# Column sum of a 32768 x 2048 matrix: folding each 8-row tile with wide adds, and a one-partition result

## The chip, the cores and the metric

The kernel runs on one core of one Trainium2 chip. The metric is the device time of one execution in microseconds (us), the median of several. The profile's *span* is the time from the first to the last instruction of one execution; in the profiled executions it is 1.8 to 1.9 us less than the time.

DVE is VectorE, ACT is ScalarE, PE is TensorE, SP is SyncE; "PEld" is PE's weight load, and ACTq and SPq are the queues on which ACT and SP issue transfers.

## The reference

```python
batch, seq, dim = 32, 1024, 2048          # float32

def reference(grad_output):
    return np.sum(grad_output, axis=(0, 1)).astype(np.float32)
```

The kernel has to read 268.44 MB and write 8 KB. A "row" below is one group of 128 x 2048 numbers: one row of 2048 in each of the 128 partitions of on-chip memory. There are 256 rows: 31 bulk tiles of 8, then a tail of 4 + 2 + 1, and a last row that is loaded in pieces.

## The kernel before

DVE adds the rows of a bulk tile to an accumulator one by one. The last five rows of the last bulk tile, and the tail, go to PE, which sums over partitions by a matmul with ones. PE's array is used as four groups of 32 columns, and the result comes out in four partitions.

```python
io_pool = ctx.enter_context(tc.tile_pool(name="io", bufs=3))   # three tiles of 64 KB a partition
# [cut]
for t in range(n_bulk):                                        # 31 tiles
    T = io_pool.tile([P, ROWS * D], fp32, tag="T", name=f"t{t}")
    nc.sync.dma_start(out=T[:], in_=src)                       # 8 MB
    on_pe = PE_ROWS_LAST if t == n_bulk - 1 else 0             # 5 in the last tile
    for j in range(ROWS):
        part = T[:, j * D : (j + 1) * D]
        if j >= ROWS - on_pe:
            sum_row(part)                                      # eight matmuls
        # [cut: t == 0 makes acc]
        else:
            nc.vector.tensor_add(out=acc[:], in0=acc[:], in1=part)
# [cut: the tail's 4, 2 and 1 rows by sum_row, acc after the first four]
for k in range(SPLIT):                                         # last row, 4 pieces of 512 columns
    nc.sync.dma_start(out=dst, in_=flat[row : row + P, k * W : (k + 1) * W])
    # [cut: four matmuls of 128 columns, one for each column group]
nc.scalar.copy(out=res[:, :n], in_=head[:])                    # pieces 0 to 2, copied early
nc.vector.tensor_copy(out=res[:, n:], in_=last[:])             # piece 3
rows = res[:].rearrange("(g r) c -> g r c", r=32)[:, 0, :]     # 4 partitions
nc.scalar.dma_start(out=o[:, : SPLIT - 1, :], in_=rows[:, :n].rearrange("g (k i) -> g k i", i=C))
nc.sync.dma_start(out=o[:, SPLIT - 1, :], in_=rows[:, n:])
```

## Time and profile before

| before | |
|---|---|
| time, median of 4 (range) | 630.51 us (630.03 to 630.67) |
| span of the profiled execution | 628.6 us |
| load queue's share of the 16 DMA engines' span | 98.9% |
| DVE busy | 555.0 us, 88% |

The table of DMA queues comes first. Its columns are the packets, the MB, and the time of the packets as a share of 16 engines' span. q1 carries the loads; "instruction" marks fetches of the engines' own programs.

```profile
...
## 3 DMA queue, kind: packets, MB, share of 16 engines
q1 hardware_dynamic: 5480, 268.44, 98.9%
q8 instruction: 2, 0.03, 0.0%
q14 instruction: 2, 0.02, 0.0%
q10 hardware_dynamic: 16, 0.01, 0.0%
...
```

The loads fill the DMA engines: their queue takes 98.9% of the engines' span. The groups of instructions by line (busy us and mean ns of one; then the idle time before them and what ended it) and the table of waits (us in total, times, longest) show DVE behind them:

```profile
...
L81 DVE TENSOR_TENSOR acc<-acc,t 128x2048 f32<-128x2048 f32 x241 | 552.4, 2292 | 34.9 <-DMA t<-in_grad_output_dram 27.7
...
```

```profile
...
DVE acc L81 <- DMA t<-in_grad_output_dram: 27.7, 30, 3.2
DVE acc L79 <- DMA t<-in_grad_output_dram: 21.8, 1, 21.8
...
```

DVE waits 27.7 + 21.8 = 49.5 us for loads. The timeline of DVE (start, length, then what it waited for) shows how. Three neighbouring bulk tiles:

```profile
...
139.03 18.57 DVE L81 TENSOR_TENSOR acc<-acc,t 128x2048 f32<-128x2048 f32 x8 [0.92 <-DMA t<-in_grad_output_dram]
159.30 18.57 DVE L81 TENSOR_TENSOR acc<-acc,t 128x2048 f32<-128x2048 f32 x8 [1.70 <-DMA t<-in_grad_output_dram]
178.65 18.57 DVE L81 TENSOR_TENSOR acc<-acc,t 128x2048 f32<-128x2048 f32 x8 [0.78 <-DMA t<-in_grad_output_dram]
...
```

Each starts with idle time that ends when its load lands, so the starts are landing times. The last bulk tile lands here:

```profile
...
605.31 6.95 DVE L81 TENSOR_TENSOR acc<-acc,t 128x2048 f32<-128x2048 f32 x3 [0.78 <-DMA t<-in_grad_output_dram]
...
```

And this is the end, in the timeline of all engines:

```profile
...
624.81 0.48 ACT L105 COPY res<-head 128x384 f32<-128x384 f32 x1 [622.79 <-PE head L50]
...
624.94 0.43 PE L50 MATMUL last<-tail,ones 128*32 128x128 f32 x8 [0.20 <-DMA tail<-in_grad_output_dram]
625.32 1.11 ACTq L108 DMA_DIRECT2D out_dram<-res  x1
625.44 0.29 DVE L106 COPY res<-last 128x128 f32<-128x128 f32 x1 [13.18 <-PE last L50]
625.75 0.66 SPq L111 DMA_DIRECT2D out_dram<-res  x1
...
```

The last load lands at 624.94, which releases PE. A copy of 0.29 us follows, and the last store is issued at 625.75.

The chain of work that ended last, as shares of the span by engine, lists DVE too:

```profile
...
DMA 69%; DVE 29%; issue 0%; SPq 0%; PE 0%; DVEq 0%
...
```

It has DVE because an add frees the buffer that the next load fills. That does not make DVE a limit: a load lands 39.4 us after its issue (median in the table of DMA issues), two tiles' time, so a whole tile is still queued when DVE frees a buffer.

### The profile page before, as it was taken

Reading aid. Unit: us, or ns where it says so; the run is one execution under the profiler, and the core shown is the slowest. Engines: PE = TensorE matmul, PEld = TensorE weight load, DVE = VectorE, ACT = ScalarE, POOL = GpSimd, SP = SyncE. Lnnn points to the kernel's source line nnn. Section 1 sums busy time; section 2 is a strip of 40 time slices with the busy share of each in tenths; the row PEclk is TensorE's granted clock in tenths of the full one; section 3 lists DMA queues with packets and bytes.
Section 4 is the critical chain, followed back from the end, with each engine's and each line's share of the span. In section 5 each row is a group of like instructions: output and inputs, shape, how many; then the busy total and the mean of one; then the engine's idle time right before and its main releaser. Section 6 shows DMA issues by size and latency. Waiting matters only on the chain.

```text
span 628.6 us, 874 instructions
## 1 busy us (share of the span) xinstructions
PE 16.2 (3%) x240; PEld 7.9 (1%) x240; DVE 555.0 (88%) x244; ACT 1.8 (0%) x2; POOL 0.2 (0%) x4
## 2 busy tenths in 40 slices
PE   0000000000000000000000000000000000000045
PEld 0000000000000000000000000000000000000022
DVE  0579999999899999999999999999999999999980
ACT  0000000000000000000000000000000000000000
POOL 0000000000000000000000000000000000000000
PEclk9999999999999999999999999999999999999999
DMA  9999999999999999999999999999999999999996
GB/s 400 404 463 404 463 409 459 400 467 401 463 404 463 404 463 404 463 404 463 404 463 404 463 404 463 404 463 401 467 400 467 400 467 400 467 400 467 400 418 256
DMA packets 5500, 268.50 MB, mean 427 GB/s; under 512 B 616, under 2 KB 632, under 8 KB 1144
## 3 DMA queue, kind: packets, MB, share of 16 engines
q1 hardware_dynamic: 5480, 268.44, 98.9%
q8 instruction: 2, 0.03, 0.0%
q14 instruction: 2, 0.02, 0.0%
q10 hardware_dynamic: 16, 0.01, 0.0%
HBM read 268.44 MB, written 0.01 MB: 427 GB/s over the span
## 4 chain that ended last, share of the span: by engine, by line
DMA 69%; DVE 29%; issue 0%; SPq 0%; PE 0%; DVEq 0%
DMA t<-in_grad_output_dram 63%; DVE acc L81 29%; DMA tail<-in_grad_output_dram 6%; SPq L97 0%; SPq L87 0%; PE last L50 0%; SPq L69 0%; DVE res L106 0%; DVEq L81 0%
## 5 line engine op out<-in xcount | busy, mean ns | idle before, releaser
L81 DVE TENSOR_TENSOR acc<-acc,t 128x2048 f32<-128x2048 f32 x241 | 552.4, 2292 | 34.9 <-DMA t<-in_grad_output_dram 27.7
L50 PE MATMUL head<-t,ones 128*32 128x384 f32 x40 | 6.5, 723 | 605.4 <-DMA t<-in_grad_output_dram 605.4
L79 DVE TENSOR_TENSOR acc<-t 128x2048 f32<-128x2048 f32 x1 | 2.3, 2291 | 21.8 <-DMA t<-in_grad_output_dram 21.8
L106 DVE COPY res<-last 128x128 f32<-128x128 f32 x1 | 0.3, 291 | 13.2 <-PE last L50 13.2
L50 PEld LDWEIGHTS head<-t,ones 128*32 128x32 f32 x40 | 1.8, 156 | 605.3 <-DVE acc L81 605.3
L50 PE MATMUL head<-tail,ones 128*32 128x384 f32 (+1 forms) x80 | 7.1, 428 | 3.6 <-DMA tail<-in_grad_output_dram 3.6
L50 PE MATMUL last<-tail,ones 128*32 128x128 f32 x64 | 3.2, 274 | 0.2 <-DMA tail<-in_grad_output_dram 0.2
L50 PE MATMUL last<-t,ones 128*32 128x128 f32 x40 | 2.9, 362 | 0.0
L105 ACT COPY res<-head 128x384 f32<-128x384 f32 x1 | 0.5, 478 | 622.8 <-PE head L50 622.8
L50 PEld LDWEIGHTS head<-tail,ones 128*32 128x32 f32 x80 | 2.0, 109 | 4.9 <-DMA tail<-in_grad_output_dram 4.9
L50 PEld LDWEIGHTS last<-tail,ones 128*32 128x32 f32 x64 | 2.0, 110 | 3.2 <-issue 2.7
L50 PEld LDWEIGHTS last<-t,ones 128*32 128x32 f32 x40 | 1.9, 150 | 3.4 <-issue 3.4
L105 ACT ACT_TABLE_LOAD x1 | 1.3, 1283 | 0.7 <-PEq L126 0.7
L50 PE MATMUL head<-acc,ones 128*32 128x384 f32 x8 | 0.8, 486 | 0.0
L39 DVE MEMSET ones<- 128x32 f32 x1 | 0.1, 85 | 0.8 <-PEq L126 0.8
L50 PE MATMUL last<-acc,ones 128*32 128x128 f32 x8 | 0.4, 273 | 0.0
L50 PEld LDWEIGHTS last<-acc,ones 128*32 128x32 f32 x8 | 0.3, 110 | 0.4 <-issue 0.4
L50 PEld LDWEIGHTS head<-acc,ones 128*32 128x32 f32 x8 | 0.2, 110 | 0.0
L126 POOL MEMSET const-bfloat16-1.0<- 128x1 bf16 x1 | 0.1, 102 | 0.0
L126 POOL MEMSET const-uint8-127<- 128x1 uint8 x1 | 0.1, 102 | 0.0
L126 POOL MEMSET const-float32-1.0<- 128x1 f32 x1 | 0.1, 99 | 0.0
L126 POOL MEMSET const-float32-0.0<- 128x1 f32 x1 | 0.1, 98 | 0.2 <-issue 0.2
## 6 DMA issues: line engine op xcount, KB each, us to landing
tail<-in_grad_output_dram SPq DMA_DIRECT2D x1, 4096.0 KB
tail<-in_grad_output_dram SPq DMA_DIRECT2D x1, 2048.0 KB, 34.3
tail<-in_grad_output_dram SPq DMA_DIRECT2D x1, 1024.0 KB, 36.3
tail<-in_grad_output_dram SPq DMA_DIRECT2D x4, 256.0 KB, 36.7
t<-in_grad_output_dram SPq DMA_DIRECT2D x31, 39.4
out_dram<-res ACTq DMA_DIRECT2D x1, 6.0 KB
out_dram<-res SPq DMA_DIRECT2D x1, 2.0 KB
```

Of the source, the lines that this page charges most:

```text
L39: nc.vector.memset(ones[:], 1.0)
L50: nc.tensor.matmul(dst, lhsT=ones[:], rhs=src, start=(g not in started), stop=stop, skip_group_check=True,)
L79: nc.vector.tensor_add(out=acc[:], in0=T[:, :D], in1=part)
L81: nc.vector.tensor_add(out=acc[:], in0=acc[:], in1=part)
L105: nc.scalar.copy(out=res[:, :n], in_=head[:])
L106: nc.vector.tensor_copy(out=res[:, n:], in_=last[:])
L126: nc = _bacc.Bacc("TRN2", target_bir_lowering=False, num_devices=1)
```

## The change

The intent is fewer, wider DVE instructions (a tile is folded in half in place: 8192, 4096 and 2048 columns, and then one add of 2048 to the accumulator), and a simpler end. PE sums one block of columns in each column group, so that the result lies in one partition and goes out in one store. All rows of the last bulk tile stay on DVE.

```diff
-        on_pe = PE_ROWS_LAST if t == n_bulk - 1 else 0
-        for j in range(ROWS):
-            part = T[:, j * D : (j + 1) * D]
-            [cut]
-                nc.vector.tensor_add(out=acc[:], in0=acc[:], in1=part)
+        n = ROWS * D // 2
+        while n >= D:
+            if t == 0 and n == D:
+                nc.vector.tensor_add(out=acc[:], in0=T[:, :n], in1=T[:, n : 2 * n])
+            else:
+                nc.vector.tensor_add(out=T[:, :n], in0=T[:, :n], in1=T[:, n : 2 * n])
+            n //= 2
+        if t:
+            nc.vector.tensor_add(out=acc[:], in0=acc[:], in1=T[:, :D])
 [cut]
+PIECES = ((0, 512, 1), (512, 512, 2), (1024, 512, 3), (1536, 256, 0), (1792, 256, 0))  # start, width, column group
+ones = const_pool.tile([P, 1], fp32)
+        sums.append(bank[32 * g : 32 * g + 1, :n])
+    add_row(acc[:])                       # after the tail's 4, 2 and 1 rows
+    for b, (lo, n, g) in enumerate(PIECES):
+        nc.sync.dma_start(out=dst, in_=flat[row : row + P, lo : lo + n])
+        add_piece(b, dst, stop=True)
+        if b in (0, 2, 4):
+            nc.scalar.copy(out=res[:, lo : lo + n], in_=sums[b])
+        else:
+            nc.vector.tensor_copy(out=res[:, lo : lo + n], in_=sums[b])
+    nc.sync.dma_start(out=out[None, :], in_=res)
-    [cut: four pieces, two copies and two stores from four partitions]
```

More of the change, by code (lines that the diff above doesn't have):

```diff
@@ L10 @@
 ROWS = 8
-GROUPS = 4
-SPLIT = 4
 TAIL = (4, 2, 1)
-PE_ROWS_LAST = 5
+PIECES = ((0, 512, 1), (512, 512, 2), (1024, 512, 3), (1536, 256, 0), (1792, 256, 0))
 @with_exitstack
@@ L28 @@
     R = flat.shape[0]
-    W = D // SPLIT
-    C = W // GROUPS
     n_bulk = (R // P - sum(TAIL) - 1) // ROWS
@@ L36, with add_piece, add_row @@
     psum_pool = ctx.enter_context(tc.tile_pool(name="psum", bufs=1, space=bass.MemoryType.PSUM))
-    ones = const_pool.tile([P, 32], fp32)
+    ones = const_pool.tile([P, 1], fp32)
     nc.vector.memset(ones[:], 1.0)
+    warm = const_pool.tile([1, 1], fp32)
+    nc.scalar.copy(out=warm[:], in_=ones[0:1, :])
     acc = const_pool.tile([P, D], fp32)
-    head = psum_pool.tile([P, (SPLIT - 1) * C], fp32)
-    last = psum_pool.tile([P, C], fp32)
-    res = const_pool.tile([P, SPLIT * C], fp32)
+    sums = []
+    for b, (lo, n, g) in enumerate(PIECES):
+        bank = psum_pool.tile([P, 512], fp32, tag=f"ps{b}", name=f"ps{b}")
+        sums.append(bank[32 * g : 32 * g + 1, :n])
     started = set()
-    def mm(dst, g, src, stop):
-        nc.tensor.matmul(
-            dst, lhsT=ones[:], rhs=src, start=(g not in started), stop=stop,
-            skip_group_check=True,
-        )
-        started.add(g)
-    def sum_row(src):
-        v = src.rearrange("p (k g i) -> p k g i", k=SPLIT, g=GROUPS)
-        for g in range(GROUPS):
-            q = slice(32 * g, 32 * g + 32)
-            mm(head[q, :].rearrange("p (k i) -> p k i", i=C), ("h", g), v[:, : SPLIT - 1, g, :], False)
-        for g in range(GROUPS):
-            q = slice(32 * g, 32 * g + 32)
-            mm(last[q, :], ("l", g), v[:, SPLIT - 1, g, :], False)
+    def add_piece(b, src, stop=False):
+        nc.tensor.matmul(sums[b], lhsT=ones[:], rhs=src, start=(b not in started), stop=stop)
+        started.add(b)
+    def add_row(src):
+        for b, (lo, n, g) in enumerate(PIECES):
+            add_piece(b, src[:, lo : lo + n])
     row = 0
@@ L70 @@
         row += P * ROWS
-        on_pe = PE_ROWS_LAST if t == n_bulk - 1 else 0
-        for j in range(ROWS):
-            part = T[:, j * D : (j + 1) * D]
-            if j >= ROWS - on_pe:
-                sum_row(part)
-            elif t == 0 and j == 0:
-                continue
-            elif t == 0 and j == 1:
-                nc.vector.tensor_add(out=acc[:], in0=T[:, :D], in1=part)
-            else:
-                nc.vector.tensor_add(out=acc[:], in0=acc[:], in1=part)
+        n = ROWS * D // 2
+        while n >= D:
+            if t == 0 and n == D:
+                nc.vector.tensor_add(out=acc[:], in0=T[:, :n], in1=T[:, n : 2 * n])
+            else:
+                nc.vector.tensor_add(out=T[:, :n], in0=T[:, :n], in1=T[:, n : 2 * n])
+            n //= 2
+        if t:
+            nc.vector.tensor_add(out=acc[:], in0=acc[:], in1=T[:, :D])
     T = io_pool.tile([P, ROWS * D], fp32, tag="T", name="tail")
@@ L89 @@
         for j in range(m):
-            sum_row(T[:, (at + j) * D : (at + j + 1) * D])
+            add_row(T[:, (at + j) * D : (at + j + 1) * D])
         at += m
-        if i == 0:
-            sum_row(acc[:])
-    for k in range(SPLIT):
-        dst = T[:, at * D + k * W : at * D + (k + 1) * W]
-        nc.sync.dma_start(out=dst, in_=flat[row : row + P, k * W : (k + 1) * W])
-        for g in range(GROUPS):
-            q = slice(32 * g, 32 * g + 32)
-            into = head[q, k * C : (k + 1) * C] if k < SPLIT - 1 else last[q, :]
-            mm(into, ("h" if k < SPLIT - 1 else "l", g), dst[:, g * C : (g + 1) * C], k >= SPLIT - 2)
-    o = out.rearrange("(k g i) -> g k i", k=SPLIT, g=GROUPS)
-    n = (SPLIT - 1) * C
-    nc.scalar.copy(out=res[:, :n], in_=head[:])
-    nc.vector.tensor_copy(out=res[:, n:], in_=last[:])
-    rows = res[:].rearrange("(g r) c -> g r c", r=32)[:, 0, :]
-    nc.scalar.dma_start(
-        out=o[:, : SPLIT - 1, :], in_=rows[:, :n].rearrange("g (k i) -> g k i", i=C)
-    )
-    nc.sync.dma_start(out=o[:, SPLIT - 1, :], in_=rows[:, n:])
+    add_row(acc[:])
+    res = acc[0:1, :]
+    for b, (lo, n, g) in enumerate(PIECES):
+        dst = T[:, at * D + lo : at * D + lo + n]
+        nc.sync.dma_start(out=dst, in_=flat[row : row + P, lo : lo + n])
[5 more added lines that the diff above has]
+    nc.sync.dma_start(out=out[None, :], in_=res)
 _INS = ['grad_output']
```

## The prediction

> What bounds it now: the loads. The page's table of DMA queues gives the load queue 98.9% of the 16 engines' span: 268.44 MB, mean 427 GB/s. [...]DVE is busy 88%, but follows: the table of waits has it waiting 49.5 us for loads, and in the timeline each 8-row tile's adds start 0.8 to 3.2 us after DVE ran dry, when a tile lands, and last 18.6 us. (The chain of waits shows DVE 29%: that is only the release of a buffer. A released buffer is refilled behind a whole tile still queued, 39.4 us from issue to landing, so the queue never drains.)
>
> What the change does.
> 1. Adds. Eight 2048-wide adds (2.292 us each, 2.325 start to start) become 8192, 4096, 2048 and 2048: the same elements. [...]Saving 0.75 us a tile, 23 us in all, none on the critical path: DVE waits longer for each landing. DVE stays about 550 us busy since five rows return to it.
> 2. The last bulk tile. Before, 3 of its rows went to DVE (6.95 us), 5 to PE. Now DVE folds all 8: landing 605.3 + 17.8 gives acc at about 623.1, while the single tail row lands at 622.4 and the last piece at 624.9. Slack under 2 us.
> 3. PE. It loses five warm-up rows. Before, the first rows cost 1.71 us each and, after 5.1 us of work, 0.86 us. Now PE first works when the 4-row tail lands (615.0), runs about three rows slowly there, and carries a backlog: 4 rows to 621, 2 rows to 622.7, 1 row to 623.5, acc to 624.4, the five pieces to about 625.4. I expect four column groups still to overlap, so a warm row stays at 0.86 us.
> 4. The end. Before, the last load (624.9) was followed by PE (0.47 us), a DVE copy (0.29) and a store; span 628.6. Now ACT copies pieces 0, 2 and 4 in turn; from its 0.478 us for 384 columns I estimate 0.57, 0.57 and 0.37 us, ending at 626.2 to 626.9, against a store issued at 625.75 before.
>
> Sum: loads unchanged; the end grows by 0.4 to 1.6 us. Predicted 631.5 us against 630.56, range 630.3 to 633.5. Faster by over 2%: 0.01; within 2%: 0.96; slower by over 2%: 0.03.
>
> Right if: load queue still 98.5 to 99%, 427 GB/s, last bulk tile landing at about 605.3, last piece at about 625; waits for loads up by some 20 us; mean of the 8192-wide add 8.7 us; acc finished at 623; PE rows 1.7, then 0.86 us; store issued at 626 to 627. Wrong if: landings move (loads would depend on DVE); [...]acc after 625.
>
> What would make it wrong. If one-column matmuls in four column groups do not overlap, or PE stays slow, the rows take two to four times as long: the end moves by 4 us, or (no overlap) by 15 or more, above 2%. If wide in-place adds slow the loads by sharing memory, all tiles shift. If loads get faster, everything moves, but nothing in the diff changes a bulk load.

Three things are cut from the recorded text, each place marked, because they come from no trace or run of this case: a bandwidth ceiling, a cost rule for the adds with the estimate made from it (17.8 us a tile), and a condition on the adds' rate. The changed kernel's trace shows: 17.80 us a tile (604.44 to 622.24; foreseen 17.8), 0.77 us saved a tile (18.57 before; 0.75), 22.3 us more waiting for loads (some 20) and 8.692 us for the 8192-wide add (8.7). ACT's copies, estimated at 0.57 us for 512 columns and 0.37 for 256, took 0.578 and 0.361. The sum came to 631.5 us: 630.56, nothing for the loads, and 0.4 to 1.6 us for the end.

## The result, and the profile after

| | before | after |
|---|---|---|
| time, median of 4 | 630.51 us | 629.96 us (629.78 to 630.96) |
| span of the profiled execution | 628.6 us | 628.2 us |
| DVE busy, instructions | 555.0 us, 244 | 547.6 us, 126 |
| last bulk tile lands at | 605.31 us | 604.44 us |
| last piece lands at | 624.94 us | 624.20 us |
| last store issued at | 625.75 us | 625.93 us |
| last store's issue to the end | 2.88 us | 2.32 us |

The ratio is 0.9996, 95% interval 0.9978 to 1.0013: no difference clear of noise. A ratio is the mean time of one kernel's runs over that of the other's of the same rounds, so it is not quite the ratio of the medians quoted. Executions over 1.5% slower than the fastest of the same kernel are left out of the means. The predicted time, 631.5 us, was 1.5 us too long, and the measured median lies just below the stated range.

The same views of the changed kernel. First the DMA queues:

```profile
...
## 3 DMA queue, kind: packets, MB, share of 16 engines
q1 hardware_dynamic: 5618, 268.45, 99.0%
q14 instruction: 1, 0.01, 0.0%
...
```

The load queue is as full as before. One instruction fetch is left of four: one of 8 KB on q14 is gone, and so are the two of 16 KB on q8. The groups by line, with the shapes kept apart, and DVE's wait for the loads:

```profile
...
L67 DVE TENSOR_TENSOR t<-t 128x8192 f32<-128x8192 f32 x31 | 269.5, 8692 | 71.8 <-DMA t<-in_grad_output_dram 71.8
L67 DVE TENSOR_TENSOR t<-t 128x4096 f32<-128x4096 f32 x31 | 137.2, 4425 | 1.1
L70 DVE TENSOR_TENSOR acc<-acc,t 128x2048 f32<-128x2048 f32 x30 | 68.8, 2292 | 1.0
L67 DVE TENSOR_TENSOR t<-t 128x2048 f32<-128x2048 f32 x30 | 68.8, 2292 | 1.0
...
```

```profile
...
DVE t L67 <- DMA t<-in_grad_output_dram: 71.8, 31, 21.8
...
```

The adds are as predicted: the trace has a mean of 8692 ns at 8192 columns, 4425 at 4096 and 2292 at 2048. What DVE saved became waiting, 71.8 us against 49.5. Two neighbouring bulk tiles in DVE's timeline, and then the last one with its final add:

```profile
...
236.02 15.48 DVE L67 TENSOR_TENSOR t<-t 128x8192 f32<-128x8192 f32 x3 [1.55 <-DMA t<-in_grad_output_dram]
...
256.12 8.69 DVE L67 TENSOR_TENSOR t<-t 128x8192 f32<-128x8192 f32 x1 [2.29 <-DMA t<-in_grad_output_dram]
...
```

```profile
...
604.44 15.48 DVE L67 TENSOR_TENSOR t<-t 128x8192 f32<-128x8192 f32 x3 [1.55 <-DMA t<-in_grad_output_dram]
619.95 2.29 DVE L70 TENSOR_TENSOR acc<-acc,t 128x2048 f32<-128x2048 f32 x1
...
```

The step between the first two is 20.10 us, 0.75 us over the usual 19.35. The accumulator is done at 619.95 + 2.29 = 622.24. The end, in the timeline of all engines:

```profile
...
622.42 1.05 PE L49 MATMUL ps<-acc,ones 128*1 128x512 f32 x10
...
623.28 1.63 PE L49 MATMUL ps<-tail,ones 128*1 128x512 f32 x10
...
624.20 0.20 PEld L49 LDWEIGHTS ps<-tail,ones 128*1 128x1 f32 x2 [0.24 <-DMA tail<-in_grad_output_dram]
624.34 1.57 ACT L89 COPY acc<-ps 1x512 f32<-1x512 f32 x3 [622.12 <-PE ps L49]
624.38 1.13 DVE L91 COPY acc<-ps 1x512 f32<-1x512 f32 x2 [2.14 <-PE ps L49]
625.93 0.33 SPq L92 DMA_DIRECT2D out_dram<-acc  x1
...
```

PE is through with the accumulator at 623.47. The first two pieces have landed by then and wait behind it, so their sums come together and the copies start at 624.34; the weight loads of the other three wait for their landings, the last one until 624.20. ACT's three copies then run one after another, take 1.57 us and decide when the store is issued.

The difference of the two spans (628.25 - 628.64 = -0.39 us) splits into three parts that can be read off these lines:

| part | before | after | difference | foreseen |
|---|---|---|---|---|
| landing of the last piece | 624.94 | 624.20 | -0.74 | 0 |
| from there to the last store's issue | 0.81 | 1.73 | +0.92 | about +0.5 to +1.2 |
| from there to the end of the span | 2.88 | 2.32 | -0.57 | 0 |

The middle part came as foreseen. The other two are what the experiments had to explain.

### Where the loads gained

The landing times differ in steps, not evenly. Outside the first 140 us, bulk tiles in both kernels land 19.34 to 19.36 us apart, with a few exceptions. Before: +0.92 us at the tile landing at 159.30, and +0.36 and +0.60 at 430.57 and 450.52. After: +0.75 at 256.12.

The records of single DMA packets in the trace tell why. They can be strung together, each 64 KB packet starting where one ended, into 16 chains of 248 (31 tiles times 8): the 16 engines. In each of the two kernels, 15 engines finish the bulk loads within about 0.4 us of one another and one is late. That one has lost its time at the moment of an instruction fetch of 8,192 bytes on q14:

```
          fetches within bulk loads   median of the     the late engine   late by
          at (us)                     other 15 ends at  ends at
before    143.4, 434.5                602.79            604.75            1.96
after     240.1                       602.92            603.92            1.00
```

The packets show the fetch on that engine. A load packet ends within 0.01 us of the fetch's start, the next one starts within 0.02 us of the fetch's end (the record lasts 0.31 to 0.33 us), and this next packet then takes 2.95 to 3.08 us instead of 2.42. In sum that is 0.84 us for before's first fetch and just under 1 us for the other two. (The +0.36 us at 430.57 lies 4 us ahead of the fetch at 434.5. The late engine's last packet for that tile ended on time, at 429.63, but the landing followed 0.94 us later instead of 0.57. Why is left unexplained.)

The landing of the last bulk tile follows the late engine: it comes 0.56 us after that engine's last packet in before and 0.52 us in the changed kernel, while the other 15 were done by 603.05 and 603.20. So a tile has landed only when its slowest engine has delivered. And as no gap between the packets of a chain is longer than 0.25 us, the lost time is not made up. So the working theory is:

- **F (fetches):** each fetch of program code within the load stream costs one DMA engine about 1 us (0.84 to 0.98 in the packets above), and the slowest engine sets every later landing. The wide adds halve DVE's program (282 instructions to 135 by my count, waits included; the traces hold 280 and 133 of them), and so save one fetch.

The rivals:

- **R (chance):** the two traces differ by luck.
- **M (memory traffic):** narrow adds slow the loads by sharing the memory with them. The shift would then grow tile by tile.

### The profile page after: what moved, and what is told of

It reads as the page before. It is cut to its first block, busy times and chain, and to the rows that moved or that the text cites. A ratio compares the mean times of both kernels' runs of the same rounds, so it can differ in the third digit from the quotient of the medians.

```text
span 628.2 us, 430 instructions
## 1 busy us (share of the span) xinstructions
PE 10.6 (2%) x90; PEld 3.8 (1%) x90; DVE 547.6 (87%) x126; ACT 3.0 (0%) x5; POOL 0.2 (0%) x4
## 4 chain that ended last, share of the span: by engine, by line
DMA 69%; DVE 28%; PE 2%; issue 0%; ACT 0%; SPq 0%; ACTq 0%
DMA t<-in_grad_output_dram 64%; DVE t L67 25%; DMA tail<-in_grad_output_dram 5%; DVE acc L70 4%; PE ps L49 2%; ACT acc L89 0%; SPq L60 0%; ACTq L118 0%
## 5 line engine op out<-in xcount | busy, mean ns | idle before, releaser
L67 DVE TENSOR_TENSOR t<-t 128x8192 f32<-128x8192 f32 (+2 forms) x92 | 475.4, 5167 | 73.9 <-DMA t<-in_grad_output_dram 71.8
L70 DVE TENSOR_TENSOR acc<-acc,t 128x2048 f32<-128x2048 f32 x30 | 68.8, 2292 | 1.0
L49 PE MATMUL ps<-tail,ones 128*1 128x512 f32 (+1 forms) x80 | 10.0, 627 | 614.3 <-DMA tail<-in_grad_output_dram 614.3
L49 PEld LDWEIGHTS ps<-tail,ones 128*1 128x1 f32 x80 | 3.5, 97 | 620.3 <-issue 617.4
L89 ACT COPY acc<-ps 1x512 f32<-1x512 f32 (+1 forms) x3 | 1.5, 506 | 622.2 <-PE ps L49 622.1
L65 DVE TENSOR_TENSOR acc<-t 128x2048 f32<-128x2048 f32 x1 | 2.3, 2292 | 0.0
```

Source lines behind the costliest of these rows:

```text
L49: nc.tensor.matmul(sums[b], lhsT=ones[:], rhs=src, start=(b not in started), stop=stop)
L65: nc.vector.tensor_add(out=acc[:], in0=T[:, :n], in1=T[:, n : 2 * n])
L67: nc.vector.tensor_add(out=T[:, :n], in0=T[:, :n], in1=T[:, n : 2 * n])
L70: nc.vector.tensor_add(out=acc[:], in0=acc[:], in1=T[:, :D])
L89: nc.scalar.copy(out=res[:, lo : lo + n], in_=sums[b])
```

## The experiments

Landings are those of the last bulk tile, unless said otherwise. Nine kernels ran, all with the right result.

### Wide adds alone

The kernel before with only its adds changed. The last tile keeps its split, and end and stores are as before.

```diff
-        for j in range(ROWS):   # [cut] acc += row j
+        if on_pe:               # the last tile as before: 3 narrow adds, 5 rows on PE
+            [cut]
+            continue
+        n = ROWS * D // 2
+        while n >= D:           # fold in place, as in the changed kernel
+            [cut]
```

> The kernel before with the wide adds alone (last bulk tile, matmuls, result and stores as before). Theory F, instruction fetches: each 8 KB fetch of instructions that falls into the load stream holds one DMA engine up by about 1 us, and the slowest engine sets every later landing. The DVE stream is 133 instructions against 282, so one fetch inside the stream against two: the last bulk tile lands at 604.3 to 604.6 (before 605.31), store and end as before (2.9 us from the last store's issue), span 627.6 to 628.0, time 629.4 to 629.9. Rival M, narrow adds slow the loads through the shared memory: the same sign, but the shift grows with every tile, not in steps at fetches. Rival R, the 0.87 us was chance: landing anywhere from 604.4 to 605.5, without regard to fetches.

The q14 line of its table of DMA queues, and its last bulk tile in DVE's timeline:

```profile
...
q14 instruction: 1, 0.01, 0.0%
...
```

```profile
...
604.49 6.94 DVE L78 TENSOR_TENSOR acc<-acc,t 128x2048 f32<-128x2048 f32 x3 [1.63 <-DMA t<-in_grad_output_dram]
...
```

Measured: 629.93 us (before in the same rounds 630.29; ratio 0.9995, 0.9982 to 1.0007: the time is not clear of noise, so the evidence is the landing). One fetch, at 240.1, as in the changed kernel; the late engine ends at 603.92, 1.00 us after the median of the others; landing 604.49, where F put it. From the last store's issue to the end, 2.87 us. The span, 628.4, missed what was expected by 0.4 us. This kernel's last load packet ends 20.34 us after the late engine's last bulk packet, against 19.70 in before and 19.79 in the changed kernel, so the last piece landed at 624.73, only 0.21 us earlier than in before. The packets of the tail show why. A fetch of 16 KB on q8, taken to be of PE's program, fills a gap between two load packets (617.84 to 619.02), and two engines now end late: one at 623.65, which is the late engine with its usual 19.7 us, and one at 624.26. In before such a fetch hides: at 618.58 it holds up another engine, which ends its loads at 624.30, and the late engine ends at 624.45. No run tested the 16 KB fetch alone.

### Narrow adds with the new end

The changed kernel with eight adds of 2048 columns a tile again, on DVE in the last tile too.

```diff
-        n = ROWS * D // 2
-        while n >= D:           # [cut] fold, then acc += row 0
+        for j in range(ROWS):
+            [cut]
+            nc.vector.tensor_add(out=acc[:], in0=acc[:], in1=part)
```

> The changed kernel with eight narrow adds a tile again, all else changed. Theory F: 289 DVE instructions, two fetches in the stream, last bulk tile at 605.2 to 605.5; then acc is done 18.6 us later (623.9), the store is issued at about 627.3, store issue to end 2.3 us, span about 629.6, time about 631.4: what was predicted for the whole change. Rival M: landing about 605.3 too, but by a shift that grows tile by tile. Rival R: no relation between fetches and landings; span 628.5 to 630.

The q14 line of its table of DMA queues, and its last bulk tile in DVE's timeline:

```profile
...
q14 instruction: 2, 0.02, 0.0%
...
```

```profile
...
604.64 13.92 DVE L69 TENSOR_TENSOR acc<-acc,t 128x2048 f32<-128x2048 f32 x6 [0.78 <-DMA t<-in_grad_output_dram]
...
```

Measured: 631.16 us (ratio 1.0019, 1.0005 to 1.0032). The fetches are back, at 142.6 and 433.8, and the late engine is 1.81 us behind the median of the others. The landing, 604.64, is earlier than expected, because the other 15 engines ended at 602.26, half a microsecond earlier than in before. So R holds in part: over all traces that median lies between 602.25 and 603.09. Most of it arises in the first 140 us, where single packets run long now and then: in before, 48 of the 912 that start there take over 2.5 us, and in the changed kernel 72. Of the 3056 that follow, only the packets after the fetches do (two and one), so outside the fetches the rest of the stream nearly keeps its pace. The lag of one engine against the others in the same trace is free of that, so it is the better measure. The time is nearly what had been predicted for the whole change.

### A dose of fetches by ACT

The changed kernel with 1280 copies of one element on ACT, which is idle until the end. They add nothing to DVE's work or to the loads.

```diff
+    for _ in range(1280):
+        nc.scalar.copy(out=warm[:], in_=ones[0:1, :])
     acc = const_pool.tile([P, D], fp32)
```

> The changed kernel with 1280 more one-element copies on ScalarE, which is idle until the end; they run in the first 300 us. Theory F: 1294 ScalarE instructions, about ten fetches of 8 KB more in the load stream, each about 0.98 us on one DMA engine; if it is one and the same engine, the last bulk tile lands about 9 to 10 us later (613 to 614.5) and the time is 638 to 641; if they are spread over engines, less. Rivals M and R: no change, last bulk tile at 604 to 605.5, time 629.5 to 631.

The load and fetch lines of its table of DMA queues, and its last bulk tile in DVE's timeline:

```profile
...
q1 hardware_dynamic: 5618, 268.45, 98.1%
q14 instruction: 11, 0.09, 0.0%
...
```

```profile
...
609.66 8.69 DVE L69 TENSOR_TENSOR t<-t 128x8192 f32<-128x8192 f32 x1 [1.55 <-DMA t<-in_grad_output_dram]
...
```

Measured: 635.18 us (ratio 1.0078, 1.0064 to 1.0092). Eleven fetches, ten of them ACT's (17 to 272 us, one for every 130 or so ACT instructions). The landing moved from 604.44 to 609.66, though the added work touches four bytes of memory at a time. M and R have no room for that. The size was off, since I took the number from DVE's fetches: here the late engine ends at 609.19, 6.90 us after the median, which is 0.69 us for each ACT fetch. The packets agree: the one that follows an ACT fetch mostly takes 2.80 us, not 3.08, and 0.31 + (2.80 - 2.42) = 0.69. DVE's one fetch hit a different engine (1.24 us late), so it did not add to the total.

### A dose of fetches by DVE

The changed kernel with nine memsets of one element a partition in each bulk tile but the last, into a part of the tile that is no longer needed.

```diff
+        if t < n_bulk - 1:
+            for _ in range(9):
+                nc.vector.memset(T[:, D : D + 1], 1.0)
```

> The changed kernel with nine more one-element memsets on DVE in each bulk tile but the last, into the dead part of that tile. Theory F: 405 DVE instructions, three fetches in the stream against one, last bulk tile at 606.2 to 606.6 (after: 604.44), span about 630.1, time about 632. DVE has about 18.7 us of work a tile and still waits for each landing. Rival M (DVE's memory traffic): memsets of one element add none, landing 604.4. Rival R: 604 to 605.5.

```profile
...
q14 instruction: 3, 0.02, 0.0%
...
```

```profile
...
606.09 13.15 DVE L67 TENSOR_TENSOR t<-t 128x8192 f32<-128x8192 f32 x2 [0.55 <-DMA t<-in_grad_output_dram]
...
```

(Again the q14 line of the queues, and DVE's last bulk tile.) Measured: 632.04 us (ratio 1.0027, 1.0013 to 1.0041), against 629.96 for the changed kernel. Three fetches, at 104.3, 296.4 and 483.7; the late engine 3.34 us behind, 1.1 us a fetch. DVE still waited 43.0 us for loads, so it was not the limit.

Set out by the number of fetches that hit the late engine within the bulk loads, all kernels:

```
kernel                        fetches   late by (us)   per fetch
after                         1 (DVE)   1.00           1.00
wide adds alone               1 (DVE)   1.00           1.00
before                        2 (DVE)   1.96           0.98
narrow adds with new end      2 (DVE)   1.81           0.91
DVE dose                      3 (DVE)   3.34           1.11
ACT dose                      10 (ACT)  6.90           0.69
two stores                    1 (DVE)   1.28           1.28
store in pieces (a repeat)    1 (DVE)   1.20           1.20
before, one store             2 (DVE)   1.97           0.99
carried rows                  1 (DVE)   1.16           1.16
carried rows summed early     1 (DVE)   0.98           0.98
```

The lag also holds what that engine was ahead or behind without a fetch, so its share for one fetch scatters (0.91 to 1.28 us for DVE's; in before, the other 15 engines end between 602.65 and 603.05). Read from the packets themselves (the fetch's record and the lengthening of the next packet), a DVE fetch costs its engine 0.84 to 0.98 us in all these traces.

### The store: two of them, or its shape

The last 0.57 us was the same in every kernel with one end or the other: 2.88 and 2.87 us with before's stores, and 2.31 to 2.32 us (changed kernel, narrow adds, both doses, and the two later versions with carried rows) with the new one. So it is no chance. Before's stores differ from the new one in two ways: there are two, on two queues, and they come from four partitions in pieces of 512 bytes. The first test keeps the one partition and makes two stores of it:

```diff
-    nc.sync.dma_start(out=out[None, :], in_=res)
+    nc.scalar.dma_start(out=out[None, :1536], in_=res[:, :1536])
+    nc.sync.dma_start(out=out[None, 1536:], in_=res[:, 1536:])
```

> The changed kernel with its single 8 KB store cut in two, the first 6 KB on ScalarE's queue and the last 2 KB on SyncE's, as before had two. From the last store's issue to the end of the span, before takes 2.88 us and the changed kernel 2.32 us, and so does every kernel with the one or the other ending so far. If the second store is the cost: back to 2.8 to 2.9 us. If the cost is the four source partitions and 512-byte pieces of the store: stays at 2.3 us. Span 0 to 0.6 us over the changed kernel's, time 630 to 630.6.

The end of this kernel, in the timeline of all engines:

```profile
...
624.58 1.18 ACT L89 COPY acc<-ps 1x512 f32<-1x512 f32 x2 [622.37 <-PE ps L49]
...
625.79 0.49 ACTq L92 DMA_DIRECT2D out_dram<-acc  x1
626.33 0.36 ACT L89 COPY acc<-ps 1x256 f32<-1x256 f32 x1 [0.57 <-ACT acc L89]
626.71 0.33 SPq L93 DMA_DIRECT2D out_dram<-acc  x1
...
```

Measured: 630.39 us (629.68 to 630.65; ratio 0.9999). From the last issue to the end of the span (628.87) is 2.16 us, so a second store alone does not bring the 0.57 us back. It cost elsewhere: ACT spends 0.49 us on issuing its store, and its last copy waits behind that.

A second test was to keep one store, cut into 512-byte pieces.

```diff
-    nc.sync.dma_start(out=out[None, :], in_=res)
+    nc.sync.dma_start(out=out.rearrange("(o a b) -> o a b", o=1, b=128), in_=res.rearrange("p (a b) -> p a b", b=128))
```

> The changed kernel with one store still, but in 16 pieces of 512 bytes. If pieces cost: the issue takes longer than 0.33 us and the end comes later than 2.32 us after the issue (2.6 to 2.9). If only a second store costs: 2.3 us.

This told nothing about pieces. The 16 pieces are contiguous and were merged, and the built program has the same instructions as the changed kernel's. It serves as a repeat: 629.86 us against 630.22 for before in the same rounds (ratio 0.9994, 0.9980 to 1.0007, again not clear of noise), one fetch at 240.1, landing 604.42 (604.44 the first time), 2.31 us after the store's issue.

The third test takes before and makes its two stores one, from the same four partitions:

```diff
-    nc.scalar.dma_start(out=o[:, : SPLIT - 1, :], in_=rows[:, :n].rearrange("g (k i) -> g k i", i=C))
-    nc.sync.dma_start(out=o[:, SPLIT - 1, :], in_=rows[:, n:])
+    nc.sync.dma_start(out=o, in_=rows.rearrange("g (k i) -> g k i", i=C))
```

> The kernel before with its two stores (6 KB on ScalarE's queue, 2 KB on SyncE's) made one on SyncE's queue, from the same four partitions in the same 512-byte pieces. Last store's issue to the end of the span was 2.88 us with the two, and 2.32 us with one store from one partition. If the four partitions and pieces cost it: 2.8 to 3.0 us. If the second queue costs it: 2.3 to 2.4 us and the issue itself still 0.6 to 1.1 us long. The loads as in before: two fetches, last bulk tile at 604.6 to 605.5; span 628.0 to 628.9; time 630.0 to 630.7.

```profile
...
626.10 0.70 SPq L108 DMA_DIRECT2D out_dram<-res  x1
...
```

(The line is its store in the timeline.) Measured: 630.55 us (before in the same rounds 630.25; ratio 1.0002). The span ends at 629.12, 3.02 us after the issue, and the issue itself takes 0.70 us against 0.33. So the 0.57 us does not need a second queue, and a second queue alone does not bring it. SP's semaphore waits in the traces divide it. SP has the completion of its last store 1.41 us after the issue in the changed kernel, 1.79 us in before and 1.94 us here: 0.38 us of the 0.57 go with the shape of the store, 0.33 of them as its longer issue. Which half of the shape, four partitions or scattered pieces, stays open. The rest, 0.18 us, comes after the store is done, in the closing instructions of the program (0.91 us in the changed kernel, 1.09 in before, 1.07 here); that it too comes from the store was not shown. The loads repeat before's: two fetches, at 143.6 and 434.8, the late engine 1.97 us behind.

### Two tries at a faster version

If fetches cost, fewer DVE instructions should help further. This version has three adds a tile (8192, 4096, 4096): two rows are carried from tile to tile, and PE sums both at the end.

```diff
-        [cut: the fold of the changed kernel]
+        nc.vector.tensor_add(out=T[:, : 4 * D], in0=T[:, : 4 * D], in1=T[:, 4 * D :])
+        if carry is not None:
+            nc.vector.tensor_add(out=T[:, : 2 * D], in0=T[:, : 2 * D], in1=carry)
+        nc.vector.tensor_add(out=T[:, : 2 * D], in0=T[:, : 2 * D], in1=T[:, 2 * D : 4 * D])
+        carry = T[:, : 2 * D]
 [cut]
-    add_row(acc[:])
+    add_row(carry[:, :D])
+    add_row(carry[:, D:])
```

> The changed kernel with three adds a tile, not four, of the same elements (8192, 4096, 4096): two rows are carried from tile to tile, and the matmuls sum them at the end, one row more. The DVE program is 103 instructions, [...]against 135. Theory F: no fetch inside the load stream, so all 16 engines end their bulk loads together and the last bulk tile lands about 1 us earlier than with one fetch: 602.9 to 603.8 (after 604.44); end gains less, as the PE has one row more (0.86 us): span 627.2 to 628.0, time 629.0 to 629.8. If one fetch is needed whatever the count: landing 604.0 to 604.7, span 628.5.

Measured: 630.96 us (ratio 1.0015, 1.0003 to 1.0028), not faster. The hoped-for absence of a fetch did not come. There is one at 312.2 us, when DVE has executed 47 instructions, and that is exactly the count at which it came in the changed kernel (47, at 240.1 us). So the first fetch came at the same count in both programs, of 103 and 135 instructions; in before, of 282, it came at 58, and the next 135 instructions later, at 193. What I had built on, that a program as short as this needs no fetch, was wrong. The landing is 603.97, and the late engine 1.16 us behind. The end lost what was left: the pieces' matmuls start 0.93 us later than in the changed kernel (624.21 against 623.28), and one row more on PE is about 0.86 us. (A 16 KB fetch fell at 622.9, but the last load packet still ended the usual 19.78 us after the late engine's bulk loads.)

The other version adds to this that four rows of the last bulk tile go to PE, so that the carried rows are summed before the tail lands.

```diff
-        nc.vector.tensor_add(out=T[:, : 4 * D], in0=T[:, : 4 * D], in1=T[:, 4 * D :])
+        if t == n_bulk - 1:
+            for j in (4, 5, 6, 7):
+                add_row(T[:, j * D : (j + 1) * D])
+        else:
+            nc.vector.tensor_add(out=T[:, : 4 * D], in0=T[:, : 4 * D], in1=T[:, 4 * D :])
 [cut: the two add_row of the carried rows move ahead of the tail]
```

> The same, and four rows of the last bulk tile go to the PE again, so that DVE is done 9 us after its landing and the carried rows are summed before the tail lands. No fetch: last bulk tile at 602.9 to 603.8. The PE is warm and without backlog when the five pieces land, so the copies start earlier and the store is issued about 1.3 us after the last load (after: about 2.2 us). Span 626.2 to 627.2, time 628.0 to 629.0: faster than both. If the PE's own fetch (seen in before at 303 PE instructions executed; here about 287 in all) falls into the tail, 0.5 to 1 us of that is lost.

Copies and store of this version, in the timeline of all engines:

```profile
...
623.66 0.58 ACT L91 COPY acc<-ps 1x512 f32<-1x512 f32 x1 [621.44 <-PE ps L49]
...
624.12 1.13 DVE L93 COPY acc<-ps 1x512 f32<-1x512 f32 x2 [11.27 <-PE ps L49]
...
624.74 0.97 ACT L91 COPY acc<-ps 1x512 f32<-1x512 f32 x2 [0.50 <-PE ps L49]
625.73 0.33 SPq L94 DMA_DIRECT2D out_dram<-acc  x1
...
```

Measured: 629.84 us (ratio 0.9995, 0.9982 to 1.0007): level with the changed kernel, and not clear of before either. The first copy starts 0.68 us earlier than in the changed kernel, but the store is issued only 0.20 us earlier. The last load packet ended at 623.89, later than the changed kernel's 623.71, although the bulk loads had ended 0.5 us earlier. A fetch of 16 KB at 618.7 lies in between, and, as with the wide adds alone, two engines end late: the late one at 623.17, 19.8 us after its bulk loads, and another at 623.89. That the fetch is the cause was not tested alone. No version tried beats both kernels by more than noise.

## Why the prediction was right or wrong

**Right: the loads bound the kernel, and DVE's saving buys no time of its own.** The load queue stayed full (98.9%, then 99.0%) and DVE's waits for loads rose by 22 us (some 20 predicted). The chance of 0.96 for a result within 2% was well placed.

**Right: the sizes on DVE and PE.** The 8192-wide add took 8.692 us (8.7), a tile's adds 17.8 us from landing to the finished accumulator (17.8), and DVE was busy for 547.6 us (about 550). One-column matmuls in four column groups overlap: the accumulator's ten matmul records last 0.38 or 0.59 us each (means of the groups by line, 256 and 512 columns), 5.1 us in sum, and all are done in 1.05 us.

**Right: the end up to the store's issue.** Foreseen was a store issued 0.5 to 1.2 us later, with the loads unmoved. It came 0.18 us later, with the last load 0.74 us earlier, so 0.92. Within it, PE's backlog was foreseen too large: PE was through with the accumulator at 623.5, not 624.4, and waited for the last three pieces.

**Wrong: "loads unchanged", and "nothing in the diff changes a bulk load".** This is the step that failed. The prediction's own test for this, "landings move", came true, though not for the reason it gave: the loads still do not depend on DVE's adds. The diff changes no load, but it takes instructions off DVE, and their fetches travel on the DMA engines that carry the loads (each starts within 0.01 us of the end of a load packet). Before has two fetches of DVE's program within the stream and the changed kernel one. Each holds one engine up by about 1 us (0.84 to 0.98), and the stream, at 98.9 and 99.0% of the engines' span, has no slack to hide it. The late engine's lag fell from 1.96 to 1.00 us, while the other 15 engines ended 0.13 us later, which is within their scatter from trace to trace: together 0.83 of the 0.87 us by which the last bulk tile landed earlier. The ACT dose, which gives the loads nothing to do but fetches, moved the landing by 5.2 us. The 0.74 us by which the last piece landed earlier need one thing more. With the wide adds alone it was 0.21 us, as in the tail, by the packets, a 16 KB fetch held another engine up; the changed kernel, whose PE program is shorter (90 matmul records, before 240), has no such fetch. This second part is read from the traces and was not tested alone.

**Wrong: the store's time after its issue, taken to be unchanged.** It shrank from 2.88 to 2.32 us. Of this 0.38 us belong to the store: one row from one partition is issued in 0.33 us and not 0.66, and is complete a little sooner after that. The other 0.18 us lie in the closing instructions, and their cause stays open. Both recur in the other kernels that have the same end.

The loss at the end came as foreseen, and these two unforeseen gains outweighed it. With them the prediction's sum closes: 631.5 - 0.74 - 0.57 is 630.2, against 629.96. The narrow-add variant, which has the fetches back, took 631.16 us.

**Too narrow: the range.** The term "loads" was given no spread. From trace to trace the median end of the 15 other engines' bulk loads alone lies between 602.25 and 603.09 us, a scatter of 0.84 us that comes mostly from the first 140 us of the stream. A range with its lower end at 630.3, 0.2 us below the old median, left no room for it.

## What to carry to other kernels

Where the loads fill all DMA engines, count what else rides on them: the engines' own programs are fetched over the same engines, and here every 130 or so instructions of DVE cost one DMA engine 0.84 to 0.98 us. The whole kernel pays when that is the engine that ends last (in the ACT dose, DVE's fetch hit another, which was 1.24 us late where the last was 6.90, and added nothing). So fewer, wider instructions can be worth a little even on an engine that is waiting: here 0.8 us at the landing of the last bulk tile, and nothing in the time that is clear of noise. When a load-bound kernel moves by less than a microsecond, look at the landing times tile by tile for steps, and compare the slowest DMA engine with the others of the same trace, which takes run-to-run scatter out.

## What the traces show of fetches and of a small store

- A fetch of DVE's program did not hold up DVE (before's eight adds across the fetch at 143.4 took 18.57 us, as elsewhere), but it held up the full load stream: 0.84 to 0.98 us per DVE fetch and mostly 0.69 us per ACT fetch on one DMA engine, and the kernel's time with it (ten ACT fetches: 635.18 us against 629.96).
- DVE's and ACT's fetches show as records of 8,192 bytes, about every 130 instructions, the first in DVE's stream after 47 to 58. Only those on q8 have 16,384 bytes. They are taken to be PE's: kernels whose traces hold 187 PE records have none of them, those with 208 and 287 have one, and those with 487 two.
- Each fetch on q14 in the load stream starts within 0.01 us of the end of a load packet. Its record lasts 0.31 to 0.33 us, but the loads on its engine are put back by about 0.7 us (ACT) to 1 us (DVE), because the next load packet runs long: 2.80 us (ACT) and 2.95 to 3.08 us (DVE) instead of 2.42. Why it does stays open.
- A small store by its shape: from one partition, 8 KB was complete 1.41 us after its issue (issue 0.33 us), and from four partitions in 512-byte pieces the last store was complete after 1.79 to 1.94 us (issue 0.66 to 0.70 us).
